# First norm of a fused diffusion block: five modulation columns on TensorE, their weights right behind x

## The chip, the cores and the metric

The kernel runs on one core of one Trainium2 chip. The time is the device time of one execution in microseconds (us), given as the median of a few runs. Engines: PE is TensorE (PEld its weight loads), DVE VectorE, ACT ScalarE, POOL GpSimd, SP SyncE, which issues nearly all loads and stores.

## The reference

One layer over 1024 latent tokens and 256 context tokens, width 1024. Each norm is modulated by columns that come from a condition vector (`c` for the latents, `c_ctx` for the context):

```python
cond_lat = jax.nn.silu(c)
cond_ctx = jax.nn.silu(c_ctx)[None, :]
m_l = jnp.split(cond_lat @ ada_w[i] + ada_b[i], N_MOD, axis=-1)   # N_MOD = 9, 1024 each
m_c = jnp.split(cond_ctx @ ada_w[i] + ada_b[i], N_MOD, axis=-1)
x = x + 0.5 * m_l[2][:, None, :] * swiglu(modulate(rms_norm(x, norm1_w[i]), m_l[0], m_l[1]),
                                            ffn1_w1[i], ffn1_w3[i], ffn1_w2[i])
...   # the same for ctx; token mixing; a second feed-forward; a last norm

def modulate(h, shift, scale):
    return h * (1.0 + scale[:, None, :]) + shift[:, None, :]
```

So the first norm needs `m_l[0]` (shift) and `m_l[1]` (scale) before the first feed-forward product can start.

## The kernel before, in words

Everything is held transposed: features on the 128 partitions, tokens along the free axis, in tiles of 128x512. A vector of 1024 features is eight columns of 128. The 9 x 8 = 72 modulation columns are numbered: 0 to 7 shift the first norm, 8 to 15 scale it, and so on; `mod[0]` holds them for the latents, `mod[1]` for the context. Products are made in three parts, from a high and a low half of each operand (`mm3`, L424 to L426: `hh` x `whi`, `hl` x `whi`, `hh` x `wlo`).

The change lies in `first1`, the start of the kernel: the first norm of the first 512 latent tokens and the first products of the feed-forward. TensorE, VectorE and ScalarE run there strictly in the order in which the code is written; SyncE issues its loads in that order too. In the code's order before:

- `warm(34)` gives TensorE 34 products of a tile of ones with itself, whose result nobody reads (L1137), while x is loaded. `squares` sums the squares of the eight pieces of x as they land (ScalarE L533 and L536, VectorE L537, into `nacc`).
- `cond` loads the row `c`, broadcast to all partitions, and makes its silu (L451, L452). `mod_load(8)` and `mod_load(0)` load the weights of columns 8 and 0 (`adaT`, 128x1024, 512 KB each).
- `rstd_col` (L546, a one-column sum on TensorE, then VectorE L1524 and GpSimd L1525) makes the norm's factor for each token, `warm(8)` eight more idle products, `mod_sum(8)` column 8 on VectorE (L486: weights times condition row, summed; `mod_fin` L513 then makes `1 + scale` times the norm's weight). `rstd_rows` (L553, L562) and a copy (L1157) spread the factor over all partitions (`nrb`). `mod_sum(0)` makes column 0.
- Then a loop over the eight feature blocks, `st`. `norm_a` makes x times column 8 + `st` times `nrb` (L576) and, with the shift column `st` added, the high half `hh` (ScalarE L577); `norm_b` makes the low half `hl` (L582). Each step then gives its three products to each of up to six chains (four in `psa`, two in `psb`), whose weights `load` brings in and splits (SyncE L620, ScalarE L1122, VectorE L1126). The modulation columns of the next step are made in between.
- Columns 1 and 2 are not made by VectorE but by TensorE: `shift_load` loads the weights in another arrangement (`adaN`, L457), `shift_col` makes eight products with the two condition columns `ccol` (L462; in the trace each is two instructions, so 16), which gives the column for latents and context at once, and `shift_out` adds the bias on ScalarE (two instructions, L467).

The weights of the columns go through five buffers in turn. The context's columns and the rest of the latents' are made on VectorE later, beside the second part of the feed-forward (`todo` in `run`, from `EMODS`).

Of the kernel before, what the change touches and what calls it, by code (L numbers as in the profile page):

```python
# [13 lines left out]
AF = mybir.ActivationFunctionType  # L14
# [3 lines left out]
P = 128  # L18
D = 1024
KD = D // P  # L20
# [370 lines left out]
class Trunk:  # L391
# [50 lines left out]
    def cond(self):  # L442
        self.cs = [self.cond_row("c")]
        self.junk = self.tile(self.dp, [P, D], mybir.dt.bfloat16, "junk")
        self.ada, self.ab = -1, tuple(range(AB))

    def cond_row(self, name, tag=None):
        nc = self.nc
# [3 lines left out]
            nc.scalar.activation(t[:, o:o + 512], t[:, o:o + 512], AF.Silu)  # L452
        return t

    def shift_load(self, j):
        t = self.ada_tile()
        self.nc.sync.dma_start(t, self.I["adaN"][j - 1])  # L457
        return t

    def shift_col(self, j, t):  # L460
        for k in range(KD):
            self.nc.tensor.matmul(self.shift[:, 2 * j:2 * j + 2], t[:, k * P:(k + 1) * P], self.ccol[:, 2 * k:2 * k + 2],  # L462
                                  start=k == 0, stop=k == KD - 1)

    def shift_out(self, j):
        for s in range(2):
            self.nc.scalar.activation(self.mod[s][:, j:j + 1], self.shift[:, 2 * j + s:2 * j + s + 1], AF.Identity,  # L467
                                      bias=self.col("ada_b")[:, j:j + 1])

    def ada_tile(self):  # L470
        self.ada += 1
# [636 lines left out]
    def first1(self, pools, n1):  # L1108
# [26 lines left out]
        def warm(n):  # L1135
            for _ in range(n):
                nc.tensor.matmul(idle[:, :P], self.ones, self.ones, start=True, stop=True)  # L1137

        def chains(st):
            for i in sorted(pss):  # L1140
                products(i, (st,))

        self.ndg, idle = 4, self.psA()
        warm(WARM[0])
        acc = self.squares(self.x[0], 512, n1)
        self.cond()
        cur = [self.mod_load(8), self.mod_load(0)]
        raw = [high(*i) for i in FIRST[-1]]
        r = self.rstd_col(acc, 512, n1)
        warm(WARM[1])  # L1150
        self.mod_sum(8, cur[0], (0,), True)
        pr = self.rstd_rows(r, 512, n1)
        for i, w in zip(FIRST[-1], raw):
            low(*i, w)
        self.mod_sum(0, cur[1], (0,), True)
        rb[0] = self.scr(n1, "nrb")
        nc.scalar.copy(rb[0], pr)  # L1157
        self.shift = self.psB()
        acc, pss = None, {}
        sh = self.shift_load(1)  # L1160
        for st in range(KD):
            self.norm_a(0, st, a, b, rb[0], n1, self.x[0][st])
            if st == 0:
                self.shift_col(1, sh)
                self.shift_out(1)
            if st == 1:
                self.shift_out(2)
            if st + 1 < KD:
                self.mod_col(9 + st, (0,), True)
                if st >= SH:  # L1170
                    self.mod_col(st + 1, (0,), True)
            if st == KD - 1:
                load(6, 0), load(6, 1)
            self.norm_b(0, st, b, self.x[0][st])
            if st in X1:
                self.load_x(pools, (1,), X1[st])
            if st in SQ:
                acc = self.squares(self.x[1], 512, n1, "", SQ[st], acc)
            for i, _ in FIRST[-1]:
                if i not in pss:  # L1180
                    pss[i] = self.psA()
# [697 lines left out]
    def run(self):  # L1879
# [18 lines left out]
        warm = self.tile(self.dp, [P, 64], F32, "warm")[:, :8]  # L1898
# [6 lines left out]
        n1 = opn("n1")  # L1905
# [41 lines left out]
        for at, (tg, k) in zip(xat, ((tg, 4 * q + k) for tg, q in ((0, 0), (1, 1), (0, 1), (1, 0)) for k in range(4))):  # L1947
            o = TGS[tg][0]
# [95 lines left out]
        A = self.bank4(self.psA)  # L2044
# [33 lines left out]
        for tg in LATTG:  # L2078
            o, n = TGS[tg]
# [84 lines left out]
def layout(inputs):  # L2164
# [8 lines left out]
    A["adaN"] = c(g["ada_w"][0][:, P:(SH + 1) * P].reshape(KD, P, SH, P).transpose(2, 1, 0, 3)).reshape(SH, P, D)  # L2173
# [67 lines left out]
```

## Time and profile before

| | |
|---|---|
| time, median of 3 runs | 2101.93 us (2101.53 to 2105.65) |
| the profiled execution | 2104.49 us, its span 2102.4 us |
| TensorE busy | 2079.4 us, 99% of the span |
| VectorE busy | 1482.6 us, 71% |
| ScalarE busy | 963.4 us, 46% |
| GpSimd busy | 203.8 us, 10% |
| mean granted TensorE clock | 0.995 |
| the first 60 us | TensorE busy 51.96 us, granted clock 0.89, DMA 309 GB/s |

A row of the timeline has: start and duration in us, engine, line of the kernel, instruction, tile written <- tiles read, shapes, how many are merged in the row, and in brackets how long the engine stood idle before it and what ended that. SPq is SyncE's queue. In the view by stretches a row has the stretch (from:to in us), its length, the busy time and the number of instructions of each engine asked for, then the clock granted to TensorE (1.00 is full), the busy share of the DMA engines and GB/s. The end of a TensorE instruction is modelled, so one overlaps the next; starts are what to count by.

### The profile page before, as it was taken

To read this page: it belongs to the slowest core of one execution; us is meant where nothing else is said; L and a number is where in the kernel's file an instruction comes from. 1 tells how busy PE (TensorE), PEld (TensorE's weight loads), DVE (VectorE), ACT (ScalarE), POOL (GpSimd) and SP (SyncE) were. 2 spreads that over 40 slices of the span, in tenths; PEclk is the share of its full clock that TensorE was granted. 3 is DMA by queue.
4 is the path that set the end of the run, shared out by engine and by line. 5 is a ranking of instruction groups with operands and counts; after the bars stand their busy time and mean duration, and the time that the engine had idled before them with its cause. 6 is when DMAs were issued, how large, how long until landed. Compare 5 with 4: busy or idle time off the path is not lost.

```text
span 2102.4 us, 34392 instructions
## 1 busy us (share of the span) xinstructions
PE 2079.4 (99%) x12490; PEld 1782.8 (85%) x12490; DVE 1482.6 (71%) x2682; ACT 963.4 (46%) x1791; POOL 203.8 (10%) x195
## 2 busy tenths in 40 slices
PE   8999999999999999999999999999999999999998
PEld 7888888888889999999789988888788888888888
DVE  7889999866776445764777368867766676665686
ACT  4433433435544445664764246444434334344553
POOL 0000000000016664001011001000000000000000
PEclk8999999999999999999999999999999999999999
DMA  9267867549886553663222223252244444477674
GB/s 342 86 213 236 286 216 254 197 159 355 290 290 225 181 186 104 207 194 97 83 82 85 77 73 110 91 172 70 92 164 138 153 167 149 149 234 236 221 235 147
DMA packets 201242, 370.36 MB, mean 176 GB/s; under 512 B 24144, under 2 KB 37104, under 8 KB 201072
## 3 DMA queue, kind: packets, MB, share of 16 engines
q1 hardware_dynamic: 200640, 368.03, 53.2%
q8 instruction: 98, 1.61, 0.3%
q14 instruction: 72, 0.59, 0.1%
q10 hardware_dynamic: 432, 0.13, 0.0%
HBM read 293.59 MB, written 66.09 MB: 171 GB/s over the span
## 4 chain that ended last, share of the span: by engine, by line
PE 92%; DVE 3%; DMA 2%; issue 1%; ACT 1%; SPq 1%; POOL 0%; ACTq 0%; DVEq 0%; POOLq 0%
PE psa L147 16%; PE psa L424 13%; PE psa L426 13%; PE psa L425 13%; PE psb L426 10%; PE psb L425 10%; PE psb L424 10%; PE psb L147 6%; DMA raw<-in_w 1%; DMA ada<-in_adaN 0%; DVE hl L582 0%; DMA hl<-sd 0%; DVE wlo L420 0%; DVE junk L486 0%; PE psb L562 0%
## 5 line engine op out<-in xcount | busy, mean ns | idle before, releaser
L419 ACT ACTIVATE whi<-raw 128x512 fp32r<-128x512 f32 x403 | 254.0, 631 | 526.8 <-issue 158.9
L420 DVE TENSOR_TENSOR wlo<-raw,whi 128x512 fp32r<-128x512 f32 x403 | 276.7, 688 | 182.8 <-ACT whi L419 179.5
L424 PE MATMUL psa<-hh,whi 128*128 128x512 f32 x772 | 302.3, 392 | 0.1
L425 PE MATMUL psa<-hl,whi 128*128 128x512 f32 x772 | 301.6, 391 | 0.0
L426 PE MATMUL psa<-hh,wlo 128*128 128x512 f32 x772 | 301.6, 391 | 0.0
L424 PE MATMUL psb<-hh,whi 128*128 128x512 f32 x632 | 246.1, 389 | 0.6 <-ACT whi L419 0.5
L425 PE MATMUL psb<-hl,whi 128*128 128x512 f32 x632 | 246.2, 390 | 0.5 <-DVE hl L420 0.5
L426 PE MATMUL psb<-hh,wlo 128*128 128x512 f32 x632 | 246.1, 389 | 0.6 <-DVE wlo L420 0.6
L424 PEld LDWEIGHTS psa<-hh,whi 128*128 128x128 f32 x772 | 145.5, 189 | 31.1 <-ACT s L668 0.5
L426 PEld LDWEIGHTS psa<-hh,wlo 128*128 128x128 f32 x772 | 145.4, 188 | 30.2 <-DVE wlo L420 0.2
L425 PEld LDWEIGHTS psa<-hl,whi 128*128 128x128 f32 x772 | 145.5, 188 | 29.9
L420 POOL TENSOR_TENSOR hl<-s,hh 128x512 fp32r<-128x512 f32 x88 | 138.3, 1598 | 138.6 <-DVE hl L420 80.7
L425 PEld LDWEIGHTS psb<-hl,whi 128*128 128x128 f32 x632 | 118.6, 188 | 26.1 <-DVE hl L420 1.6
L424 PEld LDWEIGHTS psb<-hh,whi 128*128 128x128 f32 x632 | 118.6, 188 | 26.0 <-ACT whi L419 1.0
L426 PEld LDWEIGHTS psb<-hh,wlo 128*128 128x128 f32 x632 | 118.6, 188 | 25.8 <-DVE wlo L420 1.2
L147 PE MATMUL psa<-hh,wlo 128*128 128x512 f32 x320 | 126.7, 396 | 1.0 <-issue 1.0
L147 PE MATMUL psa<-hl,whi 128*128 128x512 f32 x320 | 127.6, 399 | 0.0
L147 PE MATMUL psa<-hh,whi 128*128 128x512 f32 x320 | 127.5, 398 | 0.0
L147 DVE TENSOR_TENSOR wlo<-raw,whi 128x512 fp32r<-128x512 f32 (+1 forms) x100 | 62.0, 632 | 82.4 <-ACT whi L147 82.2
L426 PE MATMUL psa<-hh,hl 128*128 128x256 f32 x392 | 111.1, 284 | 0.0
L424 PE MATMUL psa<-hh,hh 128*128 128x256 f32 x392 | 111.1, 283 | 0.0
L425 PE MATMUL psa<-hl,hh 128*128 128x256 f32 x392 | 110.9, 283 | 0.0
(406 smaller groups left out, 4692.0 us busy)
## 6 DMA issues: line engine op xcount, KB each, us to landing
raw<-in_w SPq DMA_DIRECT2D x242, 256.0 KB, 3.3
s<-in_w SPq DMA_DIRECT2D x198, 256.0 KB, 3.8
gd<-s SPq DMA_DIRECT2D x154, 256.0 KB, 2.8
ada<-in_adaT SPq DMA_DIRECT2D x76, 512.0 KB, 4.6
raw<-gd SPq DMA_DIRECT2D x91, 256.0 KB, 3.1
sd<-s SPq DMA_DIRECT2D x44, 256.0 KB, 2.9
raw<-sd SPq DMA_DIRECT2D x44, 256.0 KB, 3.4
hh<-in_w SPq DMA_DIRECT2D x44, 256.0 KB, 3.8
```

Source lines behind the costliest of these rows:

```text
L147: self.rec.add(self.eng, lambda: f(*map(get, a), **{x: get(v) for x, v in k.items()}), outs, ins, name, a, k)
L419: nc.scalar.activation(hi, src, AF.Copy)
L420: (eng or nc.vector).tensor_tensor(out=lo, in0=src, in1=hi.bitcast(F32), op=ALU.subtract)
L424: mm(ps, wa[0], xa[0], start=start, stop=False, skip_group_check=more)
L425: mm(ps, wa[0], xa[1], start=False, stop=False, skip_group_check=more)
L426: mm(ps, wa[1], xa[0], start=False, stop=stop, skip_group_check=more)
```

## The change

Columns 8, 0 and 9 move from VectorE to TensorE beside 1 and 2 (`PECOL`). `shift_load`, `shift_col` and `shift_out` become `pe_load`, `pe_col` and `pe_out`, which also does the column's finish (`mod_fin`, on VectorE). The weights of columns 8 and 0 are loaded right behind x, those of 9 and 1 behind the first two weight tiles, the row `c` only after those. Of idle products there are now 40, then 4 behind column 8, then 2 behind column 0, for 34 and 8 before. Since TensorE makes a column for both conditions, the context's columns 0, 8 and 9 leave the later list.

```diff
-    def shift_col(self, j, t):
+    def pe_col(self, i, t):
+        o = self.pcol[:, 2 * i:2 * i + 2]
         for k in range(KD):
-            self.nc.tensor.matmul(self.shift[:, 2 * j:2 * j + 2], t[:, k * P:(k + 1) * P], self.ccol[:, 2 * k:2 * k + 2],
-                                  start=k == 0, stop=k == KD - 1)
+            self.nc.tensor.matmul(o, t[:, k * P:(k + 1) * P], self.ccol[:, 2 * k:2 * k + 2], start=k == 0, stop=k == KD - 1)
-    def shift_out(self, j):
+    def pe_out(self, i):
+        j = PECOL[i]
         for s in range(2):
-            ...
+            self.nc.scalar.activation(self.mod[s][:, j:j + 1], self.pcol[:, 2 * i + s:2 * i + s + 1], AF.Identity,
                                       bias=self.col("ada_b")[:, j:j + 1])
+        self.mod_fin(j, 0, True)
...
         warm(WARM[0])
+        self.ada, self.ab, self.pcol = -1, tuple(range(AB)), self.psB()
+        cur = [self.pe_load(0), self.pe_load(1)]
         acc = self.squares(self.x[0], 512, n1)
-        self.cond()
-        cur = [self.mod_load(8), self.mod_load(0)]
-        raw = [high(*i) for i in FIRST[-1]]
+        self.pe_col(0, cur[0])
+        self.pe_out(0)
+        warm(WARM[1])
         r = self.rstd_col(acc, 512, n1)
-        warm(WARM[1])
-        self.mod_sum(8, cur[0], (0,), True)
+        raw = [high(*i) for i in FIRST[-1]]
+        cur += [self.pe_load(2), self.pe_load(3)]
+        self.pe_col(1, cur[1])
+        self.pe_out(1)
+        warm(WARM[2])
         pr = self.rstd_rows(r, 512, n1)
         for i, w in zip(FIRST[-1], raw):
             low(*i, w)
-        self.mod_sum(0, cur[1], (0,), True)
         rb[0] = self.scr(n1, "nrb")
         nc.scalar.copy(rb[0], pr)
-        self.shift = self.psB()
+        self.pe_col(2, cur[2])
         acc, pss = None, {}
-        sh = self.shift_load(1)
         for st in range(KD):
             self.norm_a(0, st, a, b, rb[0], n1, self.x[0][st])
             if st == 0:
-                self.shift_col(1, sh)
-                self.shift_out(1)
+                self.pe_out(2)
+                self.cond()
             if st == 1:
-                self.shift_out(2)
-            if st + 1 < KD:
-                self.mod_col(9 + st, (0,), True)
-                if st >= SH:
-                    self.mod_col(st + 1, (0,), True)
+                self.pe_out(4)
+            for j in (9 + st, st + 1):
+                if st + 1 < KD and j not in PECOL:
+                    self.mod_col(j, (0,), True)
...
             if st == 0:
                 chains(0)
+                self.pe_col(3, cur[3])
+                self.pe_out(3)
+                cur.append(self.pe_load(4))
...
             if st == 0:
-                sh = self.shift_load(2)
-                self.shift_col(2, sh)
+                self.pe_col(4, cur[4])
             else:
                 chains(st)
...
-        todo = [(8 * m + k, ctxs) for m, ctxs in EMODS for k in range(KD) if m or not 1 <= k <= SH]
+        todo = [(8 * m + k, ctxs) for m, ctxs in EMODS for k in range(KD) if 8 * m + k not in PECOL]
...
-SH = 2
+PECOL = (8, 0, 9, 1, 2)
-WARM = (34, 8)
+WARM = (40, 4, 2)
```

What this does to the order of instructions is seen at three places. TensorE from the start to the first product of chain 0, before (`psb_274` holds the columns, `ada_86` the weights of column 1):

```order
L1137 MATMUL psa_162<-ones_84 128x128 x34
L546 MATMUL psb_238<-ones_84,nacc_197 128x1 x4
L1137 MATMUL psa_162<-ones_84 128x128 x8
L562 MATMUL psb_256<-ndiag_257,ones_84 128x128
L562 MATMUL psb_256<-ndiag_260,ones_84 128x128
L562 MATMUL psb_256<-ndiag_263,ones_84 128x128
L562 MATMUL psb_256<-ndiag_266,ones_84 128x128
L462 MATMUL psb_274<-ccol_80,ada_86_275 128x2 x8
L424 MATMUL psa_294<-hh_18_118,wh_152 128x512
```

The same place after (`psb_203` holds the columns; `ada_62`, `ada_63` and `ada_78` are the weights of columns 8, 0 and 9):

```order
L1138 MATMUL psa_162<-ones_84 128x128 x40
L462 MATMUL psb_203<-ccol_80,ada_62_204 128x2 x8
L1138 MATMUL psa_162<-ones_84 128x128 x4
L547 MATMUL psb_246<-ones_84,nacc_208 128x1 x4
L462 MATMUL psb_203<-ccol_80,ada_63_206 128x2 x8
L1138 MATMUL psa_162<-ones_84 128x128 x2
L563 MATMUL psb_278<-ndiag_279,ones_84 128x128
L563 MATMUL psb_278<-ndiag_282,ones_84 128x128
L563 MATMUL psb_278<-ndiag_285,ones_84 128x128
L563 MATMUL psb_278<-ndiag_288,ones_84 128x128
L462 MATMUL psb_203<-ccol_80,ada_78_262 128x2 x8
L424 MATMUL psa_315<-hh_18_118,wh_152 128x512
```

The sum over `nacc`, which stood right behind the first idle products, now stands behind column 8 and four idle products, the norm's rows behind column 0. Next, TensorE within step 0, chain 1 to chain 4, before (chains 1, 2, 3 and 4 are `psa_295`, `psa_308`, `psa_318` and `psb_345`):

```order
L426 MATMUL psa_295<-hh_18_118,wlo_236 128x512
L424 MATMUL psa_308<-hh_18_118,whi_304 128x512
L425 MATMUL psa_308<-hl_19_119,whi_304 128x512
L426 MATMUL psa_308<-hh_18_118,wlo_305 128x512
L424 MATMUL psa_318<-hh_18_118,whi_314 128x512
L425 MATMUL psa_318<-hl_19_119,whi_314 128x512
L426 MATMUL psa_318<-hh_18_118,wlo_315 128x512
L462 MATMUL psb_274<-ccol_80,ada_98_322 128x2 x8
L424 MATMUL psb_345<-hh_18_118,s_154 128x512
```

And after (chains 1 to 4 are `psa_316`, `psa_341`, `psa_351` and `psb_376`; `ada_79` is column 1, `ada_90` column 2):

```order
L426 MATMUL psa_316<-hh_18_118,wlo_260 128x512
L462 MATMUL psb_203<-ccol_80,ada_79_264 128x2 x8
L424 MATMUL psa_341<-hh_18_118,whi_337 128x512
L425 MATMUL psa_341<-hl_19_119,whi_337 128x512
L426 MATMUL psa_341<-hh_18_118,wlo_338 128x512
L424 MATMUL psa_351<-hh_18_118,whi_347 128x512
L425 MATMUL psa_351<-hl_19_119,whi_347 128x512
L426 MATMUL psa_351<-hh_18_118,wlo_348 128x512
L462 MATMUL psb_203<-ccol_80,ada_90_333 128x2 x8
L424 MATMUL psb_376<-hh_18_118,s_154 128x512
```

Column 1 now stands between chains 1 and 2; column 2 keeps its place. Last, ScalarE from step 0's `hh` to the weights of chain 4 (`s_154`), before:

```order
L577 ACTIVATE hh_18_118<-x_10_92,modl_88 128x512
L467 ACTIVATE modl_88<-psb_274,cols_78 128x1
L467 ACTIVATE modc_89<-psb_274,cols_78 128x1
L1122 ACTIVATE whi_304<-raw_302 128x512
L1122 ACTIVATE whi_314<-raw_312 128x512
L577 ACTIVATE hh_20_120<-x_11_94,modl_88 128x512
L467 ACTIVATE modl_88<-psb_274,cols_78 128x1
L467 ACTIVATE modc_89<-psb_274,cols_78 128x1
L1122 ACTIVATE s_154<-raw_341 128x512
```

And after, from the row behind that `hh`:

```order
L467 ACTIVATE modl_88<-psb_203,cols_78 128x1
L467 ACTIVATE modc_89<-psb_203,cols_78 128x1
L451 ACTIVATE condc_308<-condc_308 128x512 x2
L467 ACTIVATE modl_88<-psb_203,cols_78 128x1
L467 ACTIVATE modc_89<-psb_203,cols_78 128x1
L1123 ACTIVATE whi_337<-raw_335 128x512
L1123 ACTIVATE whi_347<-raw_345 128x512
L578 ACTIVATE hh_20_120<-x_11_94,modl_88 128x512
L467 ACTIVATE modl_88<-psb_203,cols_78 128x1
L467 ACTIVATE modc_89<-psb_203,cols_78 128x1
L1123 ACTIVATE s_154<-raw_372 128x512
```

The outputs of column 9, the condition's silu and the outputs of column 1 now stand, in this order, between step 0's `hh` and the weights of chains 2 and 3. On VectorE the finish of column 9 stands between step 0's L576 and its L582.

More of the change, by code (lines that the diff above doesn't have):

```diff
@@ L444, in cond @@
         self.junk = self.tile(self.dp, [P, D], mybir.dt.bfloat16, "junk")
-        self.ada, self.ab = -1, tuple(range(AB))
     def cond_row(self, name, tag=None):
@@ L453, in cond_row, with pe_load @@
         return t
-    def shift_load(self, j):
+    def pe_load(self, i):
         t = self.ada_tile()
-        self.nc.sync.dma_start(t, self.I["adaN"][j - 1])
+        self.nc.sync.dma_start(t, self.I["adaN"][i])
         return t
-    def shift_col(self, j, t):
+    def pe_col(self, i, t):
+        o = self.pcol[:, 2 * i:2 * i + 2]
         for k in range(KD):
-            self.nc.tensor.matmul(self.shift[:, 2 * j:2 * j + 2], t[:, k * P:(k + 1) * P], self.ccol[:, 2 * k:2 * k + 2],
-                                  start=k == 0, stop=k == KD - 1)
-    def shift_out(self, j):
+            self.nc.tensor.matmul(o, t[:, k * P:(k + 1) * P], self.ccol[:, 2 * k:2 * k + 2], start=k == 0, stop=k == KD - 1)
+    def pe_out(self, i):
+        j = PECOL[i]
         for s in range(2):
-            self.nc.scalar.activation(self.mod[s][:, j:j + 1], self.shift[:, 2 * j + s:2 * j + s + 1], AF.Identity,
+            self.nc.scalar.activation(self.mod[s][:, j:j + 1], self.pcol[:, 2 * i + s:2 * i + s + 1], AF.Identity,
                                       bias=self.col("ada_b")[:, j:j + 1])
+        self.mod_fin(j, 0, True)
     def ada_tile(self):
@@ L1144, in first1 @@
         warm(WARM[0])
+        self.ada, self.ab, self.pcol = -1, tuple(range(AB)), self.psB()
+        cur = [self.pe_load(0), self.pe_load(1)]
         acc = self.squares(self.x[0], 512, n1)
-        self.cond()
-        cur = [self.mod_load(8), self.mod_load(0)]
+        self.pe_col(0, cur[0])
+        self.pe_out(0)
+        warm(WARM[1])
+        r = self.rstd_col(acc, 512, n1)
         raw = [high(*i) for i in FIRST[-1]]
-        r = self.rstd_col(acc, 512, n1)
-        warm(WARM[1])
-        self.mod_sum(8, cur[0], (0,), True)
+        cur += [self.pe_load(2), self.pe_load(3)]
+        self.pe_col(1, cur[1])
+        self.pe_out(1)
+        warm(WARM[2])
         pr = self.rstd_rows(r, 512, n1)
@@ L2172, in layout @@
     A["adaT"] = c(g["ada_w"][0].T).reshape(72, P, D)
-    A["adaN"] = c(g["ada_w"][0][:, P:(SH + 1) * P].reshape(KD, P, SH, P).transpose(2, 1, 0, 3)).reshape(SH, P, D)
+    A["adaN"] = c(g["ada_w"][0].reshape(KD, P, 72, P)[:, :, list(PECOL)].transpose(2, 1, 0, 3)).reshape(len(PECOL), P, D)
     A["ccol"] = c(np.stack([g["c"].reshape(KD, P), g["c_ctx"].reshape(KD, P)]).transpose(2, 1, 0)).reshape(P, 2 * KD)
```

## The prediction

> **What bounds the kernel now.** I read the page first, then TensorE's waits, VectorE's load and TensorE's clock by stretches, then the timeline of the first 40 us. The page:
>
> ```profile
> PE 2079.4 (99%) x12490; PEld 1782.8 (85%) x12490; DVE 1482.6 (71%) x2682; ACT 963.4 (46%) x1791; POOL 203.8 (10%) x195
> ```
>
> TensorE is busy all the time, so only what makes it idle or slow counts. Its waits from 29.5 to 800 us are three (in all, times, longest), with the timeline's row of the first:
>
> ```profile
> PE psa L425 <- DVE hl L582: 1.6, 1, 1.6
> PE psb L424 <- ACT s L1122: 1.0, 1, 1.0
> PE psb L425 <- DVE hl L420: 0.2, 1, 0.2
> ...
> 56.88 0.50 PE L425 MATMUL psa<-hl,wh 128*128 128x512 f32 x1 [1.57 <-DVE hl L582]
> ```
>
> The last big one, at 56.88, is for `hl` of step 6 of the first norm. Behind it TensorE waits 0.2 us up to 800: what moves that `hl` moves the end by as much. Ahead of it VectorE is the bound (the first row of that stretch in the timeline, and VectorE's busy time summed from 30 to 57 us):
>
> ```profile
> 30.08 1.29 DVE L1126 TENSOR_TENSOR s<-raw,s 128x512 fp32r<-128x512 f32 x2 [2.00 <-ACT s L1122]
> ...
> sum 27.00, DVE 26.54; mean DVE 4.42
> ```
>
> VectorE is full from `s<-raw,s` at 30.08, which waited for ScalarE's `s` at 29.42, to the end; 0.46 us could be made good there. Nothing behind that row is changed until that `hl`. So the prediction is one number: **when ScalarE starts `s` (L1122)**, 29.42 before.
>
> ```profile
> 19.52 3.54 PE L462 MATMUL psb<-ccol,ada 128*128 128x2 f32 x16 [0.94 <-DMA ada<-in_adaN]
> 22.92 0.77 PE L424 MATMUL psa<-hh,wh 128*128 128x512 f32 x1
> 27.23 1.84 PE L462 MATMUL psb<-ccol,ada 128*128 128x2 f32 x16
> 29.11 0.26 ACT L467 ACTIVATE modl<-psb,cols 128x1 f32<-128x1 f32 x1 [2.28 <-PE psb L462]
> 29.42 1.15 ACT L1122 ACTIVATE s<-raw 128x512 fp32r<-128x512 f32 x2
> ```
>
> Here `s` stood behind a column's output (L467), this behind the column's products (L462) on TensorE. A column takes 3.40 us of TensorE's queue (19.52 to 22.92) the first time and 1.84 the second. The difference is the clock. These stretches of 3.41 us begin where the clock changes: length, busy time of TensorE, granted clock; below the line the same for what writes `psa` alone (idle and chain products, then their weight loads), and for L462 alone:
>
> ```profile
> 12.28:15.70 3.42, 2.83 (x24) 1.00 1.04 411
> 15.70:19.11 3.41, 1.27 (x9) 1.00 1.03 406
> 19.11:22.52 3.41, 3.00 (x15) 0.50 1.04 399
> 25.94:29.35 3.41, 3.14 (x23) 1.00 0.86 317
> 29.35:32.77 3.42, 2.67 (x6) 0.50 1.05 412
> 32.77:36.18 3.41, 3.41 (x9) 0.50 1.04 391
> 36.18:39.59 3.41, 3.41 (x16) 1.00 1.03 401
> ...
> 12.28:15.70 3.42, 1.92 (x16) 1.87 (x16) 0.00 (x0) 0.00 (x0) 1.00 1.04 411
> 25.94:29.35 3.41, 1.46 (x7) 0.85 (x5) 0.00 (x0) 0.00 (x0) 1.00 0.86 317
> ...
> 25.94:29.35 3.41, 1.84 (x16) 1.00 0.86 317
> ```
>
> The clock falls at 19.11 after a stretch with 1.27 us busy. It falls again at 29.35 after one with 3.14 us busy, but of that 1.84 are column products, two output columns wide, and 1.46 wide ones. After 12.28:15.70, with 1.92 us of idle products and 0.9 of one-column sums, it stays. So it looks as if only wide products hold the clock, and about half a stretch of them is needed. It returns after 3.41 us without a gap; 2.67 (78%) were not enough at 32.77.
>
> The Trainium skill, "TensorE: Matmul & The Clock Gate", section "HAM oscillation — how this bites in real kernels", gives as its rule that TensorE must have no idle gap over about 3.4 us. The trace disagrees: its clock fell twice with no gap over 1.9 us. By the page the clock would stay at full here, which is rival A.
>
> **The change, part by part.** These rows price the stage (idle products and sums over `nacc`; then the other engines; then spacing of products at the slow and at the full clock):
>
> ```profile
> 1.04 9.96 PE L1137 MATMUL psa<-ones 128*128 128x128 f32 x68 [1.04 <-DVE mhalf L439]
> 12.87 1.05 PE L546 MATMUL psb<-ones,nacc 128*128 128x1 f32 x8 [1.87 <-DVE nacc L537]
> 13.78 2.03 PE L1137 MATMUL psa<-ones 128*128 128x128 f32 x16
> ...
> 11.46 0.63 ACT L536 ACTIVATE nsq<-x 128x512 f32<-128x512 f32 x1 [0.59 <-DMA x<-in_xT]
> 14.20 1.01 POOL L1525 TENSOR_TENSOR nr<-nr,mhalf 128x4 f32<-128x4 f32 x1 [13.37 <-DVE nr L1524]
> 18.65 0.57 ACT L1157 COPY nrb<-psb 128x512 f32<-128x512 f32 x1
> 20.59 0.75 DVE L576 SCALAR_TENSOR_TENSOR x<-x,modl,nrb 128x512 f32<-128x512 f32 x1
> 21.37 0.72 ACT L577 ACTIVATE hh<-x,modl 128x512 fp32r<-128x512 f32 x1 [2.15 <-DVE x L576]
> 22.57 0.16 DVE L513 SCALAR_TENSOR_TENSOR modl<-modl,cols 128x1 f32<-128x1 f32 x1
> 22.65 0.74 DVE L582 SCALAR_TENSOR_TENSOR hl<-x,modl,hh 128x512 fp32r<-128x512 f32 x1
> ...
> 32.82 0.63 PE L424 MATMUL psa<-hh,wh 128*128 128x512 f32 x1
> 34.10 0.63 PE L424 MATMUL psa<-hh,whi 128*128 128x512 f32 x1
> 38.51 0.39 PE L424 MATMUL psa<-hh,wh 128*128 128x512 f32 x1
> 39.19 0.39 PE L424 MATMUL psa<-hh,whi 128*128 128x512 f32 x1
> ...
> 5.00:10.00 5.00, 5.00 (x45) 5.00 (x44) 2.77 (x4) 3.55 (x7) 0.00 (x0) 1.00 0.86 283
> 15.00:20.00 5.00, 2.45 (x19) 2.10 (x17) 4.11 (x10) 1.74 (x3) 0.21 (x1) 0.91 1.04 410
> ```
>
> Prices: a chain product 1.28/3 = 0.43 us slow, 0.68/3 = 0.23 at full; an idle product 2.03/8, less the drain of the last, 0.23 at full, and twice that slow; a column 3.40 slow, 1.8 at full; the norm's rows, eight passes like those of four idle products, 0.9 at full, 8 x 0.22 = 1.76 slow (a slow pass is 3.40/16 = 0.21, 0.22 with the first).
>
> Loads. The last piece of x is there at 11.46 before, when the condition's rows stood right behind it and the DMA moved 283 GB/s in that stretch against 410 later. Column 8's weights take 0.52 MB / 410 GB/s = 1.3 us. If the condition's rows were what slowed x, x comes 5 x (1 - 283/410) = 1.5 us sooner, the weights at 11.3; if not, at 12.8. Forty idle products end 6 x 0.23 after the old 34 (11.0 less the drain), at 12.2: column 8 starts at 12.2 or 12.8. The later loads keep their order but for the condition's rows, which nothing awaits until column 10's sum.
>
> Now TensorE's queue in order, **early / late** end, in us:
>
> - Column 8 at full clock, 1.8: done 14.0 / 14.6. Four idle products, 0.92: 14.9 / 15.5. Only then the sums over `nacc`, which started at 12.87 before: 15.9 / 17.0. This is the first new cost: the norm waits behind a column.
> - The stretch that ends at 15.70 now holds 0.9 us of wide products of 3.41, where before it held 1.92. I take it that **the clock falls at 15.70**, as it did after 1.27 and 1.46, and the late end runs its sums partly slow.
> - Column 0, slow: 19.3 / 20.4. VectorE's and GpSimd's part (0.16 + 1.01 + the first diagonal) lies beside it. Two idle products 0.9: 20.2 / 21.3. Rows 1.76: 21.95 / 23.05.
> - Column 9, slow: 25.35 / 26.45. Beside it run `nrb` 0.57, `x` 0.75 and `hh` 0.72, 2.3 with the hops, hidden.
> - Column 9's output 0.26, its finish on VectorE 0.16 and `hl` 0.74, with hops 1.3: the finish now stands ahead of `hl`. First `hl` product 26.65 / 27.75; five products, 2.15: 28.8 / 29.9.
> - Column 1, slow: 32.2 / 33.3. Its two outputs stand on ScalarE ahead of the weights of chains 2 and 3: 0.35 and one `whi` of 0.65 until chain 2 starts: 33.2 / 34.3. Six products: 35.8 / 36.9.
> - Column 2, slow, and its outputs, 3.40 + 0.35: **`s` at 39.55 / 40.65**.
>
> Against 29.42 that is 10.1 or 11.2 us late. VectorE's queue holds step 1's work until then, is idle for it, and goes on full; at most 0.46 comes back. I take the early end, 10.1: the 283 of 410 GB/s lies just where the condition's rows are moved away.
>
> The rest costs nothing. Three sums and finishes less on VectorE in the first norm (L486, 1.3 us each) free time in which it now waits for TensorE. Three sums and loads less for the context later on stand in the stretch where TensorE waits 0.2 us in all, so no more can be gained. One cover is needed: the load of column 3's weights (and all behind it) now waits for column 2's tile, so it goes out 0.35 before `s`.
>
> ```profile
> ada<-in_adaT SPq DMA_DIRECT2D x15, 512.0 KB, 7.5
> 38.48 1.28 DVE L486 CUSTOM_DVE_ANT_0 junk<-ada,condc,cols 128x1024 bf16<-128x1024 f32 x1
> ```
>
> Its sum ran at 38.48, 9.1 behind `s`, and such a load took 7.5 us (median, first 60 us, queue full), so it still arrives in time, by 2 us.
>
> The profiled execution took 2104.49 us, 2.09 of it outside the span, and lies 2.56 above the median of 2101.93. The sum is a difference: 2114.6 for such an execution, and 2101.93 + 10.1 = **2112.0** as a median. What a measurement can tell from no change is 0.2%, 4.2 us.
>
> **The rivals.** *A, not slower: the clock stays at full.* If a busy TensorE of any kind holds the clock, every column costs 1.8. For it: TensorE has no gap over 1 us up to the first chain. Against it: 29.35. Then: sums done 15.9, column 0 17.7, idle products 18.2, rows 19.1, column 9 20.9, `hh` 21.4 (ahead of the column's output on ScalarE), first `hl` product 22.7, column 1 done 25.7, chain 2 from 26.7, last of chain 3 (its `wlo` decides) 28.1, column 2 29.9, `s` 30.25: 0.8 late, 1.4 at the late end, 2102.7 to 2103.3. It decides at the clock of the stretch behind 15.7.
>
> *B, the clock returns half way,* during the six products of step 0: columns 1 and 2 cost 1.6 less each and eleven products 0.2 less, 5.4 in all: 4.7 late, 2106.6. Against it: those bursts are 2.2 and 2.6 us long, and 2.67 in 29.35:32.77 did not bring it back.
>
> *C, it does not matter or gains:* x lands 1.5 us sooner and the column work hides. Then the sum ends between 1.5 below and nothing: 2100.4 to 2101.9. Against it: ScalarE's `s` stands behind column 2 in program order, and column 2 behind four others.
>
> The stretches of the clock need not lie the same in each run. The Trainium skill, same page, section "What's actually happening", says the window runs freely and does not restart with a kernel; no run shown here can tell. By my sum a fall at 13.7 instead of 15.7 adds 1.5, a fall at 17 takes 1.0 off.
>
> **How the numbers follow.** The forecast, clock down from about 15.7 to past `s`: 0.80. A 0.11, B 0.06, C 0.03. The forecast's own span is 10.1 - 1.0 to 11.2 + 1.5, so 2111.0 to 2114.6. The range takes in B and about 1 us of the runs' spread: 2105.5 to 2115.6; A, C and tails are left out, under 0.2. Slower by over 0.2% is the forecast and most of B, 0.85; within it A and most of C, 0.13; faster 0.02, as no row offers 4.2 us.
>
> **What would show it.** In the profile after: stretches behind about 15.7 at 0.50 up to some 46 us; five column groups (L462), the last four near 3.4 us; `s` near 39.6; the wait for `hl` of step 6 ending near 67. It is wrong if the last four columns take 1.8 us each (A), if the clock reads 1.00 before column 2 (B), or if TensorE, once past step 6, waits for anything new.

## The result, and the profile after

| | before | after |
|---|---|---|
| median | 2103.70 us (5 runs, 2101.53 to 2105.65) | 2117.01 us (5 runs, 2115.04 to 2118.96) |
| profiled execution | 2104.49 us, span 2102.4 | 2117.48 us, span 2115.6 |
| granted clock, mean | 0.995 | 0.991 |

The change makes the kernel slower: ratio 1.0058, 95% interval 1.0047 to 1.0068, which is 12.2 us (9.9 to 14.3). The ratio is not the quotient of the two medians, which lie 13.3 us apart. The forecast was 2112.0 with a range up to 2115.6. So the direction came out, and in the main the mechanism; the time lies 5.0 us above the forecast and 1.4 above the range. Two of the prediction's own signs of being wrong are there as well: the clock is full for one stretch before column 2, and TensorE waits longer past step 6 than it did before.

The page after, engines:

```profile
PE 2091.7 (99%) x12546; PEld 1794.9 (85%) x12546; DVE 1476.7 (70%) x2670; ACT 963.3 (46%) x1797; POOL 197.6 (9%) x195
```

TensorE has 56 more instructions and 12.3 us more busy time, and its idle time is about the same (span less busy time: 23.0 us before, 23.9 after): the time went into more and slower work, not into waiting. VectorE lost three sums in the first norm and three later (2682 to 2670 instructions, two for each sum), and the kernel is no faster for it.

The timeline after, TensorE and ScalarE in the first norm, then VectorE's first step of the full stretch and the last big wait:

```profile
12.87 2.06 PE L462 MATMUL psb<-ccol,ada 128*128 128x2 f32 x16 [1.11 <-DMA ada<-in_adaN]
16.64 1.71 PE L547 MATMUL psb<-ones,nacc 128*128 128x1 f32 x8
18.21 3.55 PE L462 MATMUL psb<-ccol,ada 128*128 128x2 f32 x16
22.62 1.91 PE L563 MATMUL psb<-ndiag,ones 128*128 128x128 f32 x8
24.32 2.05 PE L462 MATMUL psb<-ccol,ada 128*128 128x2 f32 x16
29.74 3.41 PE L462 MATMUL psb<-ccol,ada 128*128 128x2 f32 x16
36.89 3.41 PE L462 MATMUL psb<-ccol,ada 128*128 128x2 f32 x16
40.34 0.26 ACT L467 ACTIVATE modl<-psb,cols 128x1 f32<-128x1 f32 x1 [3.42 <-PE psb L462]
40.64 1.15 ACT L1123 ACTIVATE s<-raw 128x512 fp32r<-128x512 f32 x2
41.30 1.29 DVE L1127 TENSOR_TENSOR s<-raw,s 128x512 fp32r<-128x512 f32 x2 [3.14 <-ACT s L1123]
...
68.11 0.50 PE L425 MATMUL psa<-hl,wh 128*128 128x512 f32 x1 [1.60 <-DVE hl L583]
```

`s` (now L1123) starts at 40.64 instead of 29.42, 11.22 later. VectorE's `s<-raw,s` follows at 41.30 instead of 30.08, 11.22 later, and the wait for step 6's `hl` ends at 68.11 instead of 56.88, 11.23 later. The one number on which the prediction was built passes through VectorE unchanged.

The stretches of 3.41 us after (length, busy time of TensorE, its weight loads, VectorE, ScalarE, GpSimd; granted clock; DMA):

```profile
11.09:14.50 3.41, 2.30 (x21) 2.14 (x20) 1.90 (x3) 1.03 (x2) 0.00 (x0) 1.00 1.04 411
14.50:17.91 3.41, 3.41 (x18) 3.41 (x17) 0.16 (x1) 1.45 (x4) 0.00 (x0) 0.50 1.02 376
17.91:21.33 3.42, 3.42 (x18) 3.42 (x17) 1.82 (x7) 0.00 (x0) 1.01 (x1) 0.50 1.02 395
21.33:24.74 3.41, 3.41 (x18) 3.41 (x17) 0.42 (x1) 0.58 (x3) 0.00 (x0) 0.50 0.82 290
24.74:28.15 3.41, 2.53 (x18) 2.08 (x18) 1.58 (x3) 2.47 (x6) 0.00 (x0) 1.00 0.26 68
28.15:31.57 3.42, 3.42 (x15) 3.04 (x13) 0.00 (x0) 0.00 (x0) 0.00 (x0) 0.50 0.86 275
41.81:45.22 3.41, 3.41 (x9) 2.59 (x9) 3.38 (x7) 1.76 (x3) 0.00 (x0) 0.50 0.96 309
```

The clock falls at 14.50, is full again for one stretch from 24.74, behind the norm's rows (L563, 128 columns wide, 1.91 us) and the idle products, and is down again from 28.15 to 45.22. These changes lie on a grid of 3.41 us; where the grid lies in a run is called its phase below.

TensorE's waits after, 29.5 to 800 us:

```profile
PE psa L425 <- DVE hl L583: 2.4, 2, 1.6
PE psa L424 <- ACT whi L1123: 1.0, 1, 1.0
PE psb L424 <- ACT s L1123: 1.0, 1, 1.0
PE psb L425 <- DVE hl L420: 0.6, 1, 0.6
```

The last of these was 0.2 before. Past 800 us there is 0.85 more at the next norm's sums over `nacc`, and at the end the span is 13.2 us longer, not 11.2. These 2 us are a second question beside the eleven.

### The profile page after: what moved, and what is told of

It is laid out like the page before. It is cut to its first block, busy times and chain, and to the rows that moved or that the text cites. A ratio compares the mean times of both kernels' runs of the same rounds, so it can differ in the third digit from the quotient of the medians.

```text
span 2115.6 us, 34491 instructions
## 1 busy us (share of the span) xinstructions
PE 2091.7 (99%) x12546; PEld 1794.9 (85%) x12546; DVE 1476.7 (70%) x2670; ACT 963.3 (46%) x1797; POOL 197.6 (9%) x195
## 4 chain that ended last, share of the span: by engine, by line
PE 86%; DVE 5%; DMA 5%; issue 1%; ACT 1%; SPq 1%; POOL 0%; DVEq 0%; POOLq 0%; ACTq 0%
PE psa L147 14%; PE psa L424 13%; PE psa L426 13%; PE psa L425 13%; PE psb L426 9%; PE psb L425 9%; PE psb L424 9%; PE psb L147 5%; DMA raw<-in_w 1%; DMA hl<-sd 1%; DVE wlo L420 1%; DMA hl<-in_w 1%; PE psb L462 1%; DVE hl L583 0%; SPq L147 0%
## 5 line engine op out<-in xcount | busy, mean ns | idle before, releaser
L420 POOL TENSOR_TENSOR hl<-s,hh 128x512 fp32r<-128x512 f32 x88 | 131.7, 1522 | 145.4 <-ACT hh L419 140.4
```

Of the source, the lines that this page charges most:

```text
L420: (eng or nc.vector).tensor_tensor(out=lo, in0=src, in1=hi.bitcast(F32), op=ALU.subtract)
```

## Experiments

Two theories were open: that **the clock** makes the eleven (column products two output columns wide do not hold it), or that **the place** does (columns, their outputs and finishes stand in front of the chains, whatever the clock). And for the 2 us behind: the shorter later list, other places in memory, or the luck of a run. All times below were taken beside runs of the kernel before; its median was 2103.7 to 2104.3 in each set. A timeline or a stretch shows one run of its kernel, a median all of them.

### Wide column products (wide_after)

The same 40 products (80 instructions in the trace), with the two condition columns read 64 times over, so that each is 128 columns wide:

```diff
-        o = self.pcol[:, 2 * i:2 * i + 2]
+        o = self.pcol[:, P * (i % 4):P * (i % 4) + P].rearrange("p (a b) -> p a b", b=2)
...
-            self.nc.tensor.matmul(o, t[:, k * P:(k + 1) * P], self.ccol[:, 2 * k:2 * k + 2], start=k == 0, stop=k == KD - 1)
+            self.nc.tensor.matmul(o, t[:, k * P:(k + 1) * P], self.ccol[:, 2 * k:2 * k + 2].unsqueeze(1).to_broadcast([P, P // 2, 2]),
+                                  start=k == 0, stop=k == KD - 1)
```

> The changed kernel, but each column product reads its two condition columns 64 times over, so it writes 128 columns instead of 2 (the first two are used): same instructions, same order, same weight loads. Theory clock (the clock falls because two-column products do not hold it, and most of the 11.2 us is columns and products at half clock): the clock stays at 1.00 from its first rise past 45 us, all five columns take 1.8 to 2.1 us, s (L1123) starts at 30.0 to 31.5 instead of 40.6, the wait for hl of step 6 ends at 57.5 to 59 instead of 68.1, and the time is 0 to 2 us above before. Theory place (the columns and their outputs cost what they do because of where they stand in the queues, the clock is a side effect): less than 3 us better than the changed kernel, 9 us or more above before.

2108.12 us, ratio 1.0014 (1.0004 to 1.0023). The clock stayed at 1.00 from 6.75 us to 2102.5, 3.6 us before the end. Its timeline, the last column and `s`:

```profile
28.85 1.95 PE L462 MATMUL psb<-ccol,ada 128*128 128x128 f32 x16
31.14 1.15 ACT L1124 ACTIVATE s<-raw 128x512 fp32r<-128x512 f32 x2
...
58.59 0.50 PE L425 MATMUL psa<-hl,wh 128*128 128x512 f32 x1 [1.61 <-DVE hl L584]
```

A column 64 times as wide costs 1.95 us against 2.06 and 3.41. At step 6 the eleven split: 9.5 us are the clock (68.11 to 58.59), 1.7 the place (58.59 against 56.88, or 0.8 against the 57.79 of a second trace of the kernel before, below). The kernel before loses its clock for a while too; against its version with wide products (wide_before, below, 56.12) the place is 2.5. This is the case of rival A; A's sum gave `s` at 30.25 or 30.85, and it was 31.14. So `s` and step 6 fell as the first theory said, but the time fell less: it is 4.4 us above before by the medians and 2.9 by the ratio (0.8 to 4.8), where 0 to 2 was expected. So some of the loss lies behind step 6, and it is there at full clock too.

### How wide (wide_64, wide_32)

The same edit with 64 and 32 columns (`to_broadcast([P, 32, 2])`, `[P, 16, 2]`).

> The changed kernel with column products 64 output columns wide (the two columns of the condition read 32 times over), half the width that held the clock. If the clock goes by how much of TensorE's time is filled with output columns: a column's products fill half of it, and with the idle products and the chains between them that is about the 43 to 55% at which the clock fell or stayed, so it may go either way; if it falls, column products of 3.4 us and ScalarE's start of s at 36 to 40 us. If it goes by products of any width beyond a few columns: clock 1.00 up to the end of the first norm, columns 1.9 to 2.05 us, s near 31.1 us, time near 2108.

> The changed kernel with column products 32 output columns wide (the two columns of the condition read 16 times over). If the clock goes by how much of TensorE's time is filled with output columns: a quarter of a column's time is too little, the clock falls in the first 20 us as with two columns, columns of 3.4 us, s at 38 to 41 us, time 2114 to 2117. If it goes by products of any width beyond a few columns: clock 1.00 up to the end of the first norm, s near 31.1 us, time near 2108.

| output columns | first fall of the clock | `s` starts | wait for step 6 ends | median | ratio |
|---|---|---|---|---|---|
| 2 (after) | 14.50 | 40.64 | 68.11 | 2117.01 | 1.0058 (1.0047 to 1.0068) |
| 32 | 17.81 | 36.65 | 64.13 | 2115.40 | 1.0054 (1.0037 to 1.0072) |
| 64 | 23.16 | 34.71 | 62.17 | 2112.77 | 1.0034 (1.0021 to 1.0047) |
| 128 | none | 31.14 | 58.59 | 2108.12 | 1.0014 (1.0004 to 1.0023) |

The clock falls with 32 and with 64 columns too, so being wider than a few columns is not enough: of the two theories in those texts the first holds. The sizes are rough. There is one trace of each, `s` came earlier than expected with 32 and 64 columns (38 to 41 and 36 to 40), and the intervals of 2 and 32 columns overlap. Three runs have stretches that differ in little but the width. Each time TensorE was busy for the whole stretch and 1.9 us of it were column products (1.95, 1.93 and 1.87); below each stretch stands the one behind it. First 32 columns wide (wide_32):

```profile
14.40:17.81 3.41, 3.41 (x33) 3.41 (x33) 0.97 (x6) 1.28 (x4) 1.01 (x1) 1.00 1.03 406
17.81:21.22 3.41, 3.41 (x19) 3.41 (x18) 1.90 (x5) 0.87 (x3) 0.00 (x0) 0.50 1.04 402
```

Then two columns wide (outs_late, below):

```profile
14.34:17.75 3.41, 3.41 (x32) 3.41 (x32) 1.12 (x6) 1.24 (x4) 1.01 (x1) 1.00 1.04 408
17.75:21.16 3.41, 3.41 (x19) 3.41 (x18) 1.87 (x3) 0.87 (x2) 0.00 (x0) 0.50 1.03 399
```

And 128 columns wide (wide_after):

```profile
13.58:16.99 3.41, 3.41 (x33) 3.41 (x32) 0.32 (x2) 1.45 (x4) 0.30 (x1) 1.00 1.06 414
16.99:20.40 3.41, 3.41 (x33) 3.41 (x33) 2.18 (x7) 1.00 (x3) 0.71 (x1) 1.00 1.02 394
```

A TensorE that is busy without a gap loses its clock, if what it does is narrow. How much is too little shows best in wide_64, by the column products and then by what writes `psa` alone, in the stretch ahead of its fall at 23.16:

```profile
19.75:23.16 3.41, 1.31 (x12) 1.17 (x11) 1.00 1.04 410
19.75:23.16 3.41, 1.11 (x4) 0.70 (x5) 0.00 (x0) 0.00 (x0) 1.00 1.04 410
```

Counting a product of 64 columns as half a wide one, half of 1.31 and all of 1.11 make 1.76 us, 52% of the stretch, and the clock fell; the kernel before kept it with 1.92 (56%, in 12.28:15.70). These are modelled ends, so "about half" is as near as it can be said. With the rule of the Trainium skill, "TensorE: Matmul & The Clock Gate", section "HAM oscillation — how this bites in real kernels" (no idle gap over about 3.4 us), these traces disagree: the clock fell behind 14.40:17.81 and 14.34:17.75, in which TensorE had no gap at all.

### Outputs later, products narrow (outs_late)

After, with the outputs of columns 1 and 2 moved on ScalarE behind the weights of the chains that stand next:

```diff
             if st == 1:
-                self.pe_out(4)
...
-                self.pe_out(3)
...
+            if st < 2:
+                self.pe_out(3 + st)
```

> The changed kernel with two-column products as it is, but the outputs of columns 1 and 2 moved on ScalarE: column 1's behind the weights of chains 2 and 3, column 2's behind those of chains 4 and 5. Theory clock: the clock is at 0.50 as in the changed kernel and the columns stay at 3.4 us, but s need not wait for column 2 any more: it starts at 35 to 37, the wait for hl of step 6 ends at 62 to 65, 3 to 6 us below the changed kernel and still 5 us or more above before. Theory place: nearly all comes back, the wait ends by 59, at most 2 us above before.

2112.57 us, ratio 1.0035 (1.0024 to 1.0046). `s` starts at 30.51, earlier than either theory had it, since ScalarE no longer stands behind the columns; but the products still hold the queue with 3.41 us each (19.23, 26.15 and 32.12), and VectorE then waits for weights (to 44.42):

```profile
60.62 0.50 PE L425 MATMUL psa<-hl,wh 128*128 128x512 f32 x1 [1.64 <-DVE hl L583]
```

That is 3.7 late, between the two theories. This run is the fastest of its seven (2108.54 us), so the median run is likely later here. A second trace of after's first norm (after_todo, below), in which the clock fell at 16.08, was 9.3 late; here it fell at 17.75. Of the 5.6 us between 9.3 and 3.7, 1.7 are there when column 1's products start (26.15 for 27.86), ahead of the first output that was moved, and belong to the run. The other 3.9 come behind it, with the two outputs, which is an estimate from two traces. So the order in ScalarE's queue seems to make the slow clock dearer: each repair alone gives part of the time back, this one 4.4 us by the medians, the wide products 8.9.

### The kernel before with wide products (wide_before)

The same broadcast for the kernel before's two columns, nothing else.

> The kernel before, with the same widening of its two columns. Theory clock: the fall behind the second column (29.35) is gone, the columns run as before or faster, s (L1122) starts 0 to 2 us earlier than 29.42, the wait for hl of step 6 ends 0 to 2 us earlier than 56.9, time 0 to 2 us below before. Theory place: no difference, the fall at 29.35 stays.

2101.05 us, ratio 0.9984 (0.9974 to 0.9994), 2.7 us below before by the medians, a little more than expected:

```profile
28.67 1.15 ACT L1122 ACTIVATE s<-raw 128x512 fp32r<-128x512 f32 x2
...
56.12 0.50 PE L425 MATMUL psa<-hl,wh 128*128 128x512 f32 x1 [1.58 <-DVE hl L582]
```

`s` is at 28.67 instead of 29.42, and the wait for step 6 ends 0.76 earlier. A second trace of the kernel before (before_again, below) has its grid at the same place, with the first fall at 13.57 as here at 13.58; there the clock falls again at 23.81 and 30.64 and `s` starts at 30.33, here it stays full from 20.41 on. The kernel before paid for its narrow products too, only less.

### The best of both (wide_early, wide_early_end)

Wide products, the outputs late, and the norm's two steps ahead of the columns again: the sums over `nacc` before column 8, the rows before column 0, with 44 idle products ahead and none between.

```diff
-        self.pe_col(0, cur[0])
-        self.pe_out(0)
-        warm(WARM[1])
         r = self.rstd_col(acc, 512, n1)
+        self.pe_col(0, cur[0])
...
-        self.pe_col(1, cur[1])
-        self.pe_out(1)
-        warm(WARM[2])
         pr = self.rstd_rows(r, 512, n1)
...
+        self.pe_out(0)
+        self.pe_col(1, cur[1])
...
-WARM = (40, 4, 2)
+WARM = (44,)
```

> Both at once, and the sums over nacc ahead of column 8, the norm's rows ahead of column 0, the load of column 2 behind the weights of chains 2 and 3; 44 idle products in front and no others. Theory clock: clock 1.00 throughout, s at 26 to 27.5, bound by the landing of its weights and VectorE; the wait for hl of step 6 ends at 53.5 to 55, 2 to 3.5 us below before. Theory place: most of that too if the order alone decides; then the four columns may take 3.4 us and s still starts before 30.

2101.45 us, ratio 0.9986 (0.9976 to 0.9995). A second set of runs of the same kernel, for which no expectation was written, gave 2101.74 us, 0.9991 (0.9983 to 1.0000). The timeline of the first set has `s` at 25.32 and the wait for step 6 ending 3.8 earlier than before, both somewhat better than expected:

```profile
25.32 1.14 ACT L1124 ACTIVATE s<-raw 128x512 fp32r<-128x512 f32 x2
...
53.11 0.50 PE L425 MATMUL psa<-hl,wh 128*128 128x512 f32 x1 [1.59 <-DVE hl L584]
```

So with some 1.95 us for each column and the norm not behind them, the first norm is done sooner than before. Of the 3.8 us only about 2 are left at the end (2.3 and 2.0 by the medians), and the kernel before gets as much from wide products alone (2101.05 us). That moving the columns gains time is therefore not shown. One more variant put the three added columns of weights behind all other inputs, so that those might keep their places in memory:

> The kernel with wide column products and earlier sums, with the three added columns of weights in an input of their own behind all others, so that the other inputs keep their places in memory. If places in memory cost the later 2.3 us: TensorE's distance to the kernel before stays at -3.8 us from 47 to 900 us and the time is about 2100, ratio 0.998. If they don't: the distance shrinks to about -1.5 us again and the time is 2101.5, ratio 0.999.

2101.50 us, ratio 0.9991 (0.9982 to 1.0000); TensorE's distance to the kernel before went from -3.2 us at step 6 (53.72 for 56.88) to -2.5 at the next norm's `nacc` sums (852.09 for 854.58), between the two cases. The time is that of the variant without it.

### The later 2 us (after_todo, before_pad, before_again)

After with the old later list:

```diff
-        todo = [(8 * m + k, ctxs) for m, ctxs in EMODS for k in range(KD) if 8 * m + k not in PECOL]
+        todo = [(8 * m + k, ctxs) for m, ctxs in EMODS for k in range(KD) if m or not 1 <= k <= 2]
```

> The changed kernel with the kernel before's list of later columns: the context's columns 0, 8 and 9 are summed on VectorE again, so that VectorE, ScalarE and SyncE keep the order of the kernel before from the first norm on. If the shorter list costs what TensorE waits later on (waits of about 0.6 us near 652 us and 0.85 us near 866 us in the changed kernel's trace, and the drift of its distance from 11.2 us at 60 us to 13 us at the end): those two waits are gone, TensorE's distance to the kernel before stays within 0.5 us of 11.2 from 70 us to 900 us, and the time is about 2115.0, 2 us below the changed kernel. If the later drift is a matter of the run, or comes from the eleven us in the first norm: the waits stay and the time is about 2117. The wait for step 6's hl ends at 68.1 in both cases.

2116.18 us, ratio 1.0055 (1.0041 to 1.0069), the same as after. The later waits stayed (0.71 us at the `nacc` sums), so the shorter list is not their cause; three sums less later show neither a cost nor a gain. But its first norm was not that of after, though its instructions there are the same ones: the clock fell at 16.08 instead of 14.50, and the wait for step 6 did not end at 68.1, as expected in both cases:

```profile
38.76 1.15 ACT L1123 ACTIVATE s<-raw 128x512 fp32r<-128x512 f32 x2
...
66.22 0.50 PE L425 MATMUL psa<-hl,wh 128*128 128x512 f32 x1 [1.60 <-DVE hl L583]
...
157.57 0.69 DVE L754 TENSOR_TENSOR s<-s,s 128x512 f32<-128x512 f32 x1 [1.44 <-DMA s<-in_w]
272.62 0.69 DVE L754 TENSOR_TENSOR s<-s,s 128x512 f32<-128x512 f32 x1 [1.33 <-DMA s<-in_w]
```

It ends 1.9 us earlier. Of these, 0.2 came with column 8, which started at 12.66 instead of 12.87; the rest was there by column 0's start (16.36 instead of 18.21), with the later fall of the clock. The last two rows show where VectorE, nearly full in that stretch, waited for pieces of weights; that this is where it lost the 1.9 us again is not shown.

The kernel before with its repacked weights made as long as after's, no instruction changed:

```diff
-    A["adaN"] = c(g["ada_w"][0][:, P:(SH + 1) * P].reshape(KD, P, SH, P).transpose(2, 1, 0, 3)).reshape(SH, P, D)
+    A["adaN"] = c(g["ada_w"][0][:, P:6 * P].reshape(KD, P, 5, P).transpose(2, 1, 0, 3)).reshape(5, P, D)
```

> The kernel before, with the input of repacked weights made as long as in the changed kernel (five columns, of which it reads the same two), so that the inputs that stand behind it in memory may lie 1.5 MB further on; no instruction is changed. If the later waits of the changed kernel come from where the weights lie in memory: VectorE waits over 1 us for pieces of weights between 140 and 350 us, TensorE's distance to the kernel before grows by 1 to 3 us up to 900 us, and the time is 2105 to 2107. If not: the distance stays within 0.5 us up to 900 us and the time is 2103.7.

2104.15 us, ratio 1.0001 (0.9993 to 1.0010): no cost in time, as the second case has it, though TensorE's distance grew from 0.3 us at step 6 (57.17) to 1.9 at the `nacc` sums (856.45), as the first has it. The next run shows that the distance between two runs of one kernel can grow so.

The kernel before once more:

> The kernel before once more, unchanged, for a second trace of it. If the later waits of the changed kernel (VectorE waiting 1.4 us for a piece of weights near 157 us and 1.3 us near 272 us in the run with the old list, TensorE then 0.9 us near 380 us and 0.6 to 0.9 us near 652 and 866 us) are the luck of a run: this trace shows waits of that kind too, TensorE's distance to the first trace of the same kernel moves by 1 us or more between 60 and 900 us. If they belong to the changed kernels: the distance stays within 0.5 us from 60 to 900 us. Its time is 2103.7 either way, ratio 1.000, and TensorE's clock may fall at other times than 19.1, 29.4 and 930 us.

2104.55 us, ratio 1.0002 (0.9993 to 1.0010); its profiled execution took 2107.40. Its rows, VectorE's first, then TensorE's:

```profile
148.11 0.69 DVE L753 TENSOR_TENSOR s<-s,s 128x512 f32<-128x512 f32 x1 [0.57 <-DMA s<-in_w]
...
57.79 0.50 PE L425 MATMUL psa<-hl,wh 128*128 128x512 f32 x1 [1.56 <-DVE hl L582]
...
643.06 0.50 PE L425 MATMUL psb<-hl,whi 128*128 128x512 f32 x1 [0.55 <-DVE hl L420]
...
856.66 0.60 PE L546 MATMUL psb<-ones,nacc 128*128 128x1 f32 x4 [0.48 <-DVE nacc L537]
```

The first trace of the kernel before has this last group without a wait:

```profile
854.58 0.61 PE L546 MATMUL psb<-ones,nacc 128*128 128x1 f32 x4
```

And after has it here:

```profile
867.21 0.61 PE L547 MATMUL psb<-ones,nacc 128*128 128x1 f32 x4 [0.85 <-DVE nacc L538]
```

So the kernel before can have such later waits too, in another run. Against this second trace, after is 10.32 us late at step 6 (68.11 less 57.79), 10.55 at the `nacc` sums and 10.3 at the end (spans 2115.6 and 2105.3): in this pair nothing is added past the first norm. But it does not follow that the 2 us were the good luck of the first trace. That one (2104.49 us) lies 0.8 us above its kernel's median of 2103.70, and the second (2107.40) is the slowest of 11 runs, 2.9 above theirs.

Two things speak for a cost of the changed kernels behind step 6. The wait at the `nacc` sums is there in all six traces that have after's order in the first norm (0.58 to 0.85 us), in one of four with before's order (the 0.48 above), and in none of the three of wide_early's order. And each kernel's median less the end of the wait for step 6 in its trace is 2044.9 to 2047.0 us for the four sets of runs with before's order and 2047.8 to 2052.0 for the nine others. The means lie 3 us apart (2046.4 and 2049.6), the nearest two 0.8. That is an estimate, with one trace for each step 6. The shorter list (after_todo) and the places in memory (before_pad, wide_early_end) do not account for it; its cause stays open.

## Why the prediction was wrong on the size, by its own steps

The time was missed by 5.0 us in three terms of the sum: 1.8 in the median that it starts from, 1.1 in the first norm as the profiled run shows it, and 2.1 behind step 6, which the prediction put at nothing.

- **One number, `s`.** Right up to step 6: 11.22 at `s`, 11.22 on VectorE, 11.23 at step 6. None of the 0.46 us of slack came back: TensorE's wait ended 26.81 us behind VectorE's first step, against 26.80 before.
- **"What moves that `hl` moves the end by as much", and the rest costs nothing.** This is the step that failed. The end moved by 13.2 us (spans 2115.6 and 2102.4) where `hl` had moved by 11.2. I read "TensorE waits 0.2 us" off one trace as what the kernel does and gave what lies behind that `hl` no term. By the estimate from all kernels' medians above, the changed ones lose some 2 to 3 us there. What causes it stays open: the shorter list does not, and the finishes and loads were not tried by themselves.
- **The sum against a median of three.** 2101.93 was low: with 5 runs the kernel before had 2103.70, with 27 runs of a later set 2103.76. That is 1.8 of the 5.0 us. The forecast change itself, 10.1 us, lies just inside the ratio's interval (9.9 to 14.3) and 3.2 below the medians' 13.3. The range's "1 us of the runs' spread" was less than what three runs leave open.
- **The early end (10.1), because x lands 1.5 us sooner without the condition's rows.** In the profiled run this failed too. The first row is after, the squares of the last pieces of x; the second its stretch from 5 to 10 us:

```profile
10.25 2.02 ACT L537 ACTIVATE nsq<-x 128x512 f32<-128x512 f32 x3 [1.71 <-DMA x<-in_xT]
...
5.00:10.00 5.00, 5.00 (x47) 5.00 (x46) 2.77 (x4) 3.15 (x6) 0.00 (x0) 1.00 0.95 320
```

  The rate rose from 283 to 320 GB/s, but the last square ended at 12.27, before at 12.09: x came no sooner. Column 8 started at 12.87 and had waited for its weights; the late end had 12.8, the early 12.2. But that is one run. In outs_late, with the same loads up to there, the last square began at 10.50 and ended at 11.13, and column 8 started before the early end has it:

```profile
11.76 1.92 PE L462 MATMUL psb<-ccol,ada 128*128 128x2 f32 x16
```

  The last square of x ends between 11.13 and 12.27 in the six traces with these loads (mean 11.8), and between 12.09 and 12.66 in four with before's loads (mean 12.3). So x is squared sooner by some half a us on the whole, not by 1.5, and what one run shows of it is partly luck. In wide_after column 8 did not wait for weights and still began at 12.78, behind the idle products, which ran at half pace up to 6.75 us there (18 in 3.30:6.74, 31 in 6.76:10.10) and up to 4.10 in outs_late.
- **That `s` hit the late end is partly luck.** The late end had it at 40.65, and it was 40.64. By the late end the sums were to be done at 17.0 and column 0 at 20.4, and the fall at 14.50 made these about 18.2 and 21.6. Then the clock came back for 24.74:28.15, which the prediction did not have, and column 9 took 2.05 instead of 3.40, so that the first `hl` product came at 27.75, as the late end had it. In after_todo `s` started at 38.76, 0.8 before the early end.
- **The clock falls because column products are narrow.** Right, and now shown by the widths. The time, 15.70, was off (14.50, and 16.08 in the other run), and three of the last four columns took 3.4 us, not all four. That "about half a stretch" of wide products is needed fits (52% did not do).
- **A fall 2 us earlier adds 1.5, one at 17 takes 1.0 off.** Too small: 1.58 us of phase went with 1.7 us of `s` (1.88 less the 0.2 of column 8). With the kernel before's own `s` at 29.42 and 30.33 in its two traces, the lateness is 8.4 to 11.2 us by the pair of traces that one takes.
- **Rivals.** A is out (it takes wide products to have it), C is out by 13 us. B had the clock return in step 0's products; it returned behind the norm's rows and for one stretch only, columns 1 and 2 still took 3.41 us each, and `s` was 11.2 us late, not 4.7.

## What to carry to other kernels

Before work is moved to TensorE to fill its idle time, look at how many output columns it writes: products of 2, 32 and 64 columns kept the engine busy here and lost its clock, and what stands behind them in the queue then cost nearly double (a column 3.41 us for 1.95). Reading a narrow operand over and over, so that the product is 128 wide, cost no time here and kept the clock. In the kernel before, that alone gave as much as the best order of the moved columns. And when a difference of ten us is to be told in two thousand, get the kernel before's spread, of runs and of traces, before a term of one or two us is argued from one trace.

## What the runs showed of the hardware

- A column's 16 product instructions take about 1.95 us at full clock with 128 output columns, 1.90 with 64, 1.94 with 32 and 1.84 to 2.06 with two: up to 128 columns the width costs no time. Their weight loads are busy for 1.87 of 1.93 us (outs_late, 14.34:17.75), so it looks as if these set the pace.
- The clock changes on a grid of 3.41 us that lies differently in each run of the same instructions (falls at 14.50 and 16.08; in the kernel before's first two traces at 19.11 and 13.57). The Trainium skill, "TensorE: Matmul & The Clock Gate", section "What's actually happening", says that the window runs freely; the prediction could not tell, and these traces agree.
- The clock also falls for single stretches far behind: near 930 us in all three traces of the kernel before's instructions (before 930.47, before_again 931.76, before_pad 931.63), in before_pad once more at 1406.08, and not near 930 in wide_before. What decides on these falls was not looked at.
- The same loads can land 1.1 us apart or more: in after column 8 waited for its weights to 12.87, in outs_late, with the same loads up to there, it ran on them at 11.76.
